# Regrouping the readers of the transposed input, the loads of the opening, and one step of the query rotation

## The chip, the cores and the metric

The kernel runs on one core of a Trainium2 chip. The metric is the device time of one execution in microseconds, the median over several runs. The engines are TensorE (PE; weight loads are listed as PEld), VectorE (DVE), ScalarE (ACT), GpSimd (POOL), and the queues that start transfers, above all SyncE's (SP).

## The reference, cut to what matters

A two-layer encoder over 512 tokens of width 1024. Layer 0 is a combined input projection that feeds two groups of attention heads, layer 1 a neighbourhood attention; each is followed by a squared-ReLU MLP. The change lies in layer 0, in its first part:

```python
hn = rmsnorm(h, norm_mix[layer])
z = h @ w_in                                # here h is hn
qa, ka, va, cq, ckv, kr = jnp.split(z, EVEN_SPLITS, axis=-1)
qa = axial_rope(rmsnorm(qa.reshape(b, s, A_HEADS, HEAD_DIM), a_q_norm), row, col)
ka = axial_rope(rmsnorm(ka.reshape(b, s, A_KV_HEADS, HEAD_DIM), a_k_norm), row, col)
oa = block_attention(qa, ka, va, HEAD_DIM ** -0.5)
```

`rmsnorm` divides by the root of the mean square over the row; the rotation `axial_rope` mixes pairs of channels with cosine and sine tables.

## The kernel before, in words

Activations are kept channel-major: eight "row tiles" `hT[:, k, :]` of 128 channels by 512 tokens. Each fp32 matrix product is made of three single-pass products (`mm3`, lines 509 to 511): both operands are split into a rounded high part and the low remainder, and high x high, high x low and low x high are added in one PSUM bank. Splitting a weight chunk takes an ACT copy for the high part (line 212; line 210 on DVE for the first chunk) and a DVE subtraction for the low part (line 202).

**The opening.** The input x comes token-major in four column blocks (`load_x`, line 119; block 0 in two halves), each holding two row tiles. The first 384 used columns of the input projection come in eight chunks of 128 rows (`load_w`, loads at line 190, a ring of four `raw` buffers). `make_x(k)` has TensorE transpose row tile k into a PSUM bank of tag `t`, of which there are two (line 548), and then reads this bank four times: ACT rounds it times the norm's gain into the high part of `X[k]` (553), DVE makes the low part (554), ACT makes the square for the norm's sum (556), and DVE copies the tile to `hT` (557). The square is added to `acc` (560), on POOL, for the last tile on DVE. `use_w(k, m)` runs the three matmuls of row tile k and column group m; there are three groups with a bank each. Rounds k = 0 to 5 of `opening` hold the nine matmuls of tile k, and the transposes of tile k+2 among them. Then tiles 6 and 7 follow group by group (`last_rows`), with the norm's sum between (`compact_r`, line 530: products of `acc` with a column of ones), a transpose of small gain vectors (1133), and then `others`, the product for three further tiles of 128 queries. Inside `opening` the order of PE, ACT, DVE and POOL is that of the program; the SP queue's order, and all engines' before the opening, come from a planner that works with estimated times. It also makes two engines that read one PSUM bank do so one after the other, in the program's order.

**The attention of the first group.** Eight heads in pairs, four units of 128 queries each, counted by `n` in `step`. In each unit TensorE makes the scores (1004), DVE and ACT the softmax (1008, 1010), TensorE transposes the result three units later (979), ACT and DVE split that (981, 982), and after each odd unit's transposes the product with the values follows one unit later (992). Between the units `fill` puts matmuls of other products. The rotation of the next pair of query tiles comes in two steps: `rope_q` at the pair's start (POOL and SP transfers), and `sum_q`, which adds the two halves (663), splits them (665, 666) and sends parts to their partitions (667 to 669, SP). `scales` makes the norms of queries of tiles 1 to 3 from sums gathered in a staging bank of tag `t` in units 0 to 2: an ACT copy (586), four transposes (589) and sixteen small DVE operations (592 to 596, 159 to 169, 688). The order in the attention is the planner's.

Of the kernel before, what the change touches and what calls it, by code (L numbers as in the profile page):

```python
# [19 lines left out]
KD = D // P  # L20
# [10 lines left out]
def f32(ap):  # L31
    return ap.bitcast(F32)
# [3 lines left out]
def encoder_kernel(ctx: ExitStack, tc: tile.TileContext, ins, out, dbg=None):  # L36
# [54 lines left out]
    def scratch(dt=F32):  # L91
        return scp.tile([P, 512], dt, tag="sc", name=nm("sc"))
# [24 lines left out]
    def load_x(q, z=None):  # L117
        a, m = (0, 256) if z is None else (128 * z, 128)
        SP.dma_start(xq[q].t.rearrange("p (j d) -> p j d", j=4)[:, :, a : a + m],
                     xv[:, :, 256 * q + a : 256 * q + a + m])  # L120
# [12 lines left out]
    def idle_work(n, b=None):  # L133
        b = b or ob()
        for _ in range(n):
            PE.matmul(b[:, 0:P], ones, ones, start=True, stop=True)
# [8 lines left out]
    def gmix(l, k):  # L145
        return gT[:, 8 * l + k : 8 * l + k + 1]
# [36 lines left out]
    def chunk(parts, nk, ncol, heads=None, eng=None, first=False):  # L183

        raw = wp.tile([P, 1024], F32, tag="raw", bufs=4, name=nm("raw"))
        r3 = raw[:, 0 : nk * ncol].rearrange("p (k n) -> p k n", k=nk)
        for lo, n, src in parts:
            dst = r3[:, :, lo : lo + n]
            if len(src.shape) == 3:
                SP.dma_start(dst, src)  # L190
            else:
                for k in range(nk):
                    SP.dma_start(dst[:, k].rearrange("p (z m) -> p z m", z=src.shape[2]), src[:, k])
        yield
        hi = wp.tile([P, 1024], F32R, tag="whi", name=nm("whi"))
        lo_ = wp.tile([P, 1024], F32R, tag="wlo", name=nm("wlo"))
        m = nk * ncol
        v = lambda t: t[:, 0:m].rearrange("p (k n) -> p k n", k=nk)
        lows = []

        def low(to, src, high):
            z = lambda: (eng or DVE).tensor_tensor(to, src, f32(high), op=ALU.subtract)  # L202
            if eng:
                z()
            else:
                lows.append(z)

        if heads is None:
            if first:
                DVE.tensor_copy(hi[:, 0:m], raw[:, 0:m])  # L210
            else:
                ACT.activation(hi[:, 0:m], raw[:, 0:m], AF.Copy)  # L212
            low(lo_[:, 0:m], raw[:, 0:m], hi[:, 0:m])
        else:

            na, nb = heads
            hn = ncol // (na + nb)
            r4 = r3.rearrange("p k (h e) -> p k h e", h=hn)
            for e0, n, o in ((0, na, 0), (na, nb, hn * na)):
                z = [v(t)[:, :, o : o + hn * n].rearrange("p k (h e) -> p k h e", h=hn) for t in (hi, lo_)]  # L220
                src = r4[:, :, :, e0 : e0 + n]
                ACT.activation(z[0], src, AF.Copy)
                low(z[1], src, z[0])
        yield v(hi), v(lo_), lows
# [319 lines left out]
    def make_x(k):  # L544
        b = stb()
        for j in range(4):
            o = 256 * j + P * (k % 2)
            PE.transpose(b[:, j * P : (j + 1) * P], xq[k // 2].t[:, o : o + P], ident)
        order = lambda z: z.rearrange("p (c r) -> p c r", r=ROWS)
        bt = b.rearrange("p (r c) -> p c r", r=ROWS)  # L550
        x3 = X[k].t.rearrange("p (a c r) -> p a c r", a=2, r=ROWS)
        g = gmix(0, k)
        ACT.activation(x3[:, 0], bt, AF.Copy, scale=g)
        DVE.scalar_tensor_tensor(x3[:, 1], bt, g, f32(x3[:, 0]), op0=ALU.mult, op1=ALU.subtract)  # L554
        sq = acc if k == 0 else scratch()
        ACT.activation(order(sq), bt, AF.Square)
        DVE.tensor_copy(order(hT[:, k, :]), bt)
        if k:

            (DVE if k == KD - 1 else POOL).tensor_tensor(acc, acc, sq, op=ALU.add)  # L560
# [121 lines left out]
    hold = {}  # L682
# [77 lines left out]

    def load_w(k):
        w = rows(w_in, k, 1)
        _, (hi, lo, lows) = chunk([(0, 256, w[:, :, 512:768]), (256, 128, w[:, :, 0:128])], 1, 384, first=k == 0)
        for z in lows:
            z()
        W[k] = hi, lo
# [5 lines left out]
    load_x(0, 0)  # L772
    load_w(0)
    load_x(0, 1)
    load_w(1)
    load_x(1)
    make_x(0)
    idle_work(4)
    make_x(1)
    load_w(2)  # L780
    load_x(2)

    kst = Slot()

# [246 lines left out]
    def heads_A():  # L1031
        for h in range(8):
            t, e, kv = h // 2, h % 2, h // 4
            if e == 0 and t < 3:
                rope_q(t + 1)
            q, k = QA[t].pair(), KA[kv].pair()

            def done(i, t=t, e=e):
                if e == 1 and t < 3 and i == 0:
                    sum_q(t + 1)  # L1040
                if i == 3 and e:
                    QA[t].free()
                    if t % 2:
                        KA[t // 2].free()

            yield dict(e=e, done=done, scale=lambda i, h=h: scA[h][:, i : i + 1],
                       passes=lambda i, q=q, k=k, e=e: [(q[:, e, i * P : (i + 1) * P], k[:, z, :]) for z in range(2)],
                       vlhs=lambda kt, kv=kv: VAv[:, kt, kv, :], after=VA.free if h == 7 else lambda: None)
# [35 lines left out]
    def step(h, i):  # L1084
        n = count[0]
        count[0] += 1
        if n < 3:

            if n == 0:
                hold["stq"] = stb()  # L1090
            stat(hold[f"sq{n + 1}"], n, 3, ind1(n + 1)[:, 2:8], hold["stq"], 6)
            if n == 2:
                scales(hold["stq"], 6, "rsQ", 2, 6)
        if n == 35:

            ok = [s_.pair() for s_ in O]
            assert len(ok) == 4
            fill.add(*out_proj(w_out, 0, ok, [0, 1, 2], "out"))
            projB(1, True)
            fill.add(*out_proj(w_out, 0, ok, [3, 4, 5], "out"))  # L1100
            fill.add(*out_proj(w_out, 0, ok, [6, 7], "out"))
        fill.run(1.5)
# [11 lines left out]
    def opening():  # L1114
        for k in range(6):
            use_w(k, 0)
            if k == 0:
                load_x(3)
            make_x(k + 2)
            use_w(k, 1)  # L1120
            use_w(k, 2)
            if k + 3 < KD:
                load_w(k + 3)
            if k == 2:
                SP.dma_start(rpA.t, ins["cst"][:, C_ROPE : C_ROPE + 2 * S])
            if k == 3:
                preload(1)
            if k == 4:
                preload(2)
        weights(0, 0)  # L1130
        SP.dma_start(rpB.t, ins["cst"][:, C_ROPE + 2 * S : C_ROPE + 4 * S])
        gp = stb()
        PE.transpose(gp[:, 0:31], gs.t[32:63, 0:P], ident[32:63, 32:63])
        DVE.tensor_copy(gT[:, 16:47], gp[:, 0:31])

        def last_rows(m):
            for k in (6, 7):
                use_w(k, m)

        last_rows(0)  # L1140
        sqk, low_k = squares(banks[0])
        kg, sh, krot = scratch(), scratch(), Slot(F32)
        ACT.activation(kg, banks[0], AF.Copy, scale=gT[:, 46:47])
        DVE.tensor_copy(r0, compact_r(acc))
        DVE.tensor_tensor(r0sq, r0, r0, op=ALU.mult)
        last_rows(2)
        ev_q(0, banks[2])
        low_k(DVE)
        hold["low"](DVE)
        last_rows(1)  # L1150
        q0 = first_q()
        next(q0)
        va = ev_va(banks[1])
        for n, _ in enumerate(others):
            if n == 0:
                next(va)
                DVE.stream_shuffle(sh, kg, sw16)
                DVE.tensor_tensor(kg, kg, cosA, op=ALU.mult)
                DVE.tensor_tensor(sh, sh, sinA, op=ALU.mult)
                DVE.tensor_tensor(krot.t[:, 0:S], kg, sh, op=ALU.add)  # L1160
            elif n == 2:
                st = stb()
                stat(sqk, 0, 2, ind1(1)[:, 0:4], st, 4)
            elif n == 3:
                stat(hold["sq0"], 1, 2, ind1(0)[:, 0:4], st, 4)
            elif n == 5:
                rs = scales(st, 4, "rsA", 0, 2)
                ka = keys(krot, rs[:, :, 2:4])
                next(ka)
            elif n == 7:  # L1170
                next(va)
            elif n == 13:
                next(ka)
                next(q0)
                next(ka)
            elif n == 14:
                next(va)
                next(q0)
        for _ in range(3):
            next(first_z)  # L1180
# [694 lines left out]
```

## Time and profile before

| | |
|---|---|
| median of 3 runs | 1180.86 us (1178.01 to 1181.37) |
| the profiled execution | 1179.42 us, span 1177.6 us |
| mean granted TensorE clock | 0.996 |
| PE busy | 1156.2 us, 98% of the span |
| DVE busy | 898.7 us, 76% |
| ACT busy | 646.7 us, 55% |
| POOL busy | 549.6 us, 47% |

Rows of the timeline give the start, the duration, the engine, the line, the operation with its output and inputs, and in brackets how long the engine stood idle before it and what ended that. Rows of waits give the total, the number and the longest. The granted clock is a share of full speed.

### The profile page before, as it was taken

How to read it: one execution, taken by the hardware profiler on the slowest of the kernel's cores; microseconds unless marked ns; L12 is line 12 of the kernel's file. 1: busy time of each engine (PE TensorE's matmuls, PEld its weight loads, DVE VectorE, ACT ScalarE, POOL GpSimd, SP SyncE). 2: the span in 40 equal slices, each digit the busy share in tenths (PEclk: the TensorE clock that was granted, in tenths of full speed). 3: DMA queues.
4: the chain of work that ended last, by engine and by line, in shares of the span. 5: the costliest groups of instructions: out<-in, count | busy, mean ns of one | idle time of the engine just before them, and what ended most of it. 6: DMA issues, size and time to landing. Idle time of an engine off the chain costs nothing. (4 is left out here: it accounts for less than half of the span.)

```text
span 1177.6 us, 20064 instructions
## 1 busy us (share of the span) xinstructions
PE 1156.2 (98%) x7212; PEld 1021.2 (87%) x7212; DVE 898.7 (76%) x1540; ACT 646.7 (55%) x1106; POOL 549.6 (47%) x684
## 2 busy tenths in 40 slices
PE   8999999999999999999999999999999999999997
PEld 6777788888898999989998998988889899998995
DVE  6878998878876587798884676667987678779775
ACT  4667676764444456743453555555553366663344
POOL 4257242315452878429802232221357558825920
PEclk9999999999999999999999999999999999999999
DMA  7323314222435623225226465433243223342322
GB/s 207 98 73 93 90 50 135 72 64 81 149 91 174 191 76 95 89 91 162 72 73 174 126 172 137 128 105 117 90 153 108 81 73 92 90 131 75 126 73 72
DMA packets 113476, 128.04 MB, mean 109 GB/s; under 512 B 9332, under 2 KB 92193, under 8 KB 113377
## 3 DMA queue, kind: packets, MB, share of 16 engines
q1 hardware_dynamic: 110320, 119.30, 34.0%
q0 software_dynamic: 2304, 6.31, 2.3%
q8 instruction: 57, 0.93, 0.3%
q10 hardware_dynamic: 752, 1.15, 0.3%
q14 instruction: 43, 0.34, 0.1%
HBM read 104.32 MB, written 6.29 MB: 94 GB/s over the span
## 5 line engine op out<-in xcount | busy, mean ns | idle before, releaser
L312 DVE TENSOR_TENSOR wlo<-a,whi 128x896 fp32r<-128x896 f32 x133 | 164.4, 1241 | 77.3 <-ACT whi L311 74.2
L311 ACT ACTIVATE whi<-a 128x896 fp32r<-128x896 f32 x133 | 125.7, 949 | 154.1 <-PE s L397 28.1
L509 PE MATMUL mm<-a,whi 128*128 128x512 f32 x473 | 192.1, 408 | 0.8 <-ACT a L840 0.5
L510 PE MATMUL mm<-a,whi 128*128 128x512 f32 x473 | 187.6, 397 | 0.5 <-DVE a L554 0.4
L511 PE MATMUL mm<-a,wlo 128*128 128x512 f32 x473 | 187.2, 397 | 0.0
L202 DVE TENSOR_TENSOR wlo<-raw,whi 128x1024 fp32r<-128x1024 f32 (+4 forms) x117 | 136.7, 1173 | 48.9 <-ACT whi L212 46.4
L305 POOL TENSOR_TENSOR a<-a 128x128 f32<-128x128 f32 x133 | 88.2, 663 | 137.9 <-DMA a<-in_ffn_w_up_dram 74.3
L212 ACT ACTIVATE whi<-raw 128x1024 fp32r<-128x1024 f32 (+3 forms) x120 | 113.1, 945 | 66.5 <-PE s L510 18.8
L306 POOL TENSOR_TENSOR a<-a 128x256 f32<-128x256 f32 x133 | 129.0, 970 | 10.4
L307 POOL TENSOR_TENSOR a<-a 128x128 f32<-128x128 f32 x133 | 116.0, 872 | 10.4
L398 PE MATMUL mm<-a,wlo 128*128 128x256 f32 x390 | 109.6, 281 | 1.3 <-DVE wlo L312 1.3
L396 PE MATMUL mm<-a,whi 128*128 128x256 f32 x390 | 109.5, 281 | 0.0
L397 PE MATMUL mm<-a,whi 128*128 128x256 f32 x390 | 109.1, 280 | 0.0
L509 PEld LDWEIGHTS mm<-a,whi 128*128 128x128 f32 x473 | 89.2, 189 | 20.9 <-issue 1.4
L511 PEld LDWEIGHTS mm<-a,wlo 128*128 128x128 f32 x473 | 89.1, 188 | 20.5
L510 PEld LDWEIGHTS mm<-a,whi 128*128 128x128 f32 x473 | 89.5, 189 | 18.4 <-DVE a L554 1.2
L1531 POOL TENSOR_SCALAR p<-p,ti 128x256 f32<-128x256 f32 x64 | 35.6, 567 | 105.2 <-DVE ti L1530 91.8
L1012 POOL TENSOR_SCALAR p<-p,ti 128x512 f32<-128x512 f32 x64 | 45.2, 708 | 83.7 <-DVE ti L1011 66.3
L396 PE MATMUL t<-a,whi 128*128 128x256 f32 x280 | 78.6, 281 | 0.0
L397 PE MATMUL t<-a,whi 128*128 128x256 f32 x280 | 78.3, 280 | 0.0
L398 PE MATMUL t<-a,wlo 128*128 128x256 f32 x280 | 78.3, 280 | 0.0
L398 PEld LDWEIGHTS mm<-a,wlo 128*128 128x128 f32 x390 | 73.4, 188 | 2.1 <-DVE wlo L312 2.1
(354 smaller groups left out, 3260.5 us busy)
## 6 DMA issues: line engine op xcount, KB each, us to landing
a<-in_ffn_w_up_dram SPq DMA_DIRECT2D x100, 256.0 KB
raw<-in_ffn_w_down_dram SPq DMA_DIRECT2D x42, 512.0 KB
a<-in_ffn_w_down_dram SPq DMA_DIRECT2D x33, 256.0 KB
raw<-in_od_w_qkv_dram SPq DMA_DIRECT2D x64, 128.0 KB
raw<-in_ffn_w_up_dram SPq DMA_DIRECT2D x12, 512.0 KB
a<-a SPq DMA_DIRECT2D x18, 256.0 KB
bias<-bx SPq DMA_DIRECT2D x16, 256.0 KB
raw<-in_od_w_qkv_dram SPq DMA_DIRECT2D x8, 512.0 KB
```

The source lines that it names most:

```text
L202: z = lambda: (eng or DVE).tensor_tensor(to, src, f32(high), op=ALU.subtract)
L212: ACT.activation(hi[:, 0:m], raw[:, 0:m], AF.Copy)
L306: POOL.tensor_tensor(r[:, 4:6], r[:, 2:3].to_broadcast([P, 2, P]), r[:, 0:7:6], op=ALU.add)
L307: POOL.tensor_tensor(r[:, 7], r[:, 3], r[:, 5], op=ALU.subtract)
L311: ACT.activation(hi[:, 0:896], raw[:, 128:1024], AF.Copy)
L312: DVE.tensor_tensor(lo[:, 0:896], raw[:, 128:1024], f32(hi[:, 0:896]), op=ALU.subtract)
L396: PE.matmul(o, wh, x[:, 0], start=kp == 0 and n in (0, 1, 3, 5), stop=False, skip_group_check=True)
L397: PE.matmul(o, wh, x[:, 1], start=False, stop=False, skip_group_check=True)
L398: PE.matmul(o, wl, x[:, 0], start=False, stop=kp == self.np - 1, skip_group_check=True)
L509: PE.matmul(o, wh, xh, start=first, stop=False)
L510: PE.matmul(o, wh, xl, start=False, stop=False)
L511: PE.matmul(o, wl, xh, start=False, stop=last)
```

## The change

- In `make_x`, for tiles 2 to 7, the square (ACT) stands right after the rounding (ACT), ahead of DVE's two reads. For tiles 0 and 1 the square comes last and reads the copy in `hT` instead of the bank.
- Loading a weight chunk and splitting it are separate steps. Chunks 0 to 3 and all x blocks are asked for before the first split, so that chunk 3 stands ahead of x block 3; in the opening chunk k+4 is asked for in round k, where it was k+3. The load of the rotary table (line 1125) comes after round 3's weight load, instead of after round 2's.
- In round 0 the transposes of tile 2 stand behind all nine matmuls, instead of behind the first three.
- `sum_q` comes at the second unit of the pair's second head, instead of the first.
- `scales` for the query tiles 1 to 3 comes at unit 3, instead of unit 2. The staging bank is taken as before.

```diff
@@ make_x
         g = gmix(0, k)
+        sq = acc if k == 0 else scratch()
         ACT.activation(x3[:, 0], bt, AF.Copy, scale=g)
+
+        if k > 1:
+            ACT.activation(order(sq), bt, AF.Square)
         DVE.scalar_tensor_tensor(x3[:, 1], bt, g, f32(x3[:, 0]), op0=ALU.mult, op1=ALU.subtract)
-        sq = acc if k == 0 else scratch()
-        ACT.activation(order(sq), bt, AF.Square)
         DVE.tensor_copy(order(hT[:, k, :]), bt)
+        if k < 2:
+            ACT.activation(sq, hT[:, k, :], AF.Square)
@@ load_w
-        _, (hi, lo, lows) = chunk([(0, 256, w[:, :, 512:768]), (256, 128, w[:, :, 0:128])], 1, 384, first=k == 0)
+        W[k] = chunk([(0, 256, w[:, :, 512:768]), (256, 128, w[:, :, 0:128])], 1, 384, first=k == 0)
+        next(W[k])
+
+    def split_w(k):
+        hi, lo, lows = next(W[k])
         for z in lows:
             z()
         W[k] = hi, lo
@@ before the opening
     load_x(0, 1)
-    load_w(1)
-    load_x(1)
+    for k in (1, 2, 3):
+        load_w(k)
+        load_x(k)
+    split_w(0)
     make_x(0)
     idle_work(4)
+    split_w(1)
     make_x(1)
-    load_w(2)
-    load_x(2)
+    split_w(2)
@@ heads_A, done
-                if e == 1 and t < 3 and i == 0:
+                if e == 1 and t < 3 and i == 1:
                     sum_q(t + 1)
@@ step
+        if n == 0:
+            hold["stq"] = stb()
         if n < 3:
-
-            if n == 0:
-                hold["stq"] = stb()
             stat(hold[f"sq{n + 1}"], n, 3, ind1(n + 1)[:, 2:8], hold["stq"], 6)
-            if n == 2:
-                scales(hold["stq"], 6, "rsQ", 2, 6)
+        if n == 3:
+            scales(hold["stq"], 6, "rsQ", 2, 6)
@@ opening
             use_w(k, 0)
-            if k == 0:
-                load_x(3)
-            make_x(k + 2)
+            if k:
+                make_x(k + 2)
             use_w(k, 1)
             use_w(k, 2)
+            if k == 0:
+                make_x(2)
+            if k + 4 < KD:
+                load_w(k + 4)
             if k + 3 < KD:
-                load_w(k + 3)
-            if k == 2:
+                split_w(k + 3)
+            if k == 3:
                 SP.dma_start(rpA.t, ins["cst"][:, C_ROPE : C_ROPE + 2 * S])
-            if k == 3:
                 preload(1)
```

## The prediction

> **What bounds the kernel now.** I read the page's engine shares first, then TensorE's own waits, then windows over the part that the change touches, then the timeline inside those windows.
>
> ```profile
> PE 1156.2 (98%) x7212; PEld 1021.2 (87%) x7212; DVE 898.7 (76%) x1540; ACT 646.7 (55%) x1106; POOL 549.6 (47%) x684
> PE o L992 <- DVE a L982: 2.1, 3, 1.7
> PE t L548 <- DVE hT L557: 1.8, 2, 1.4
> PE t L530 <- DVE acc L560: 1.4, 1, 1.4
> PE t L1133 <- issue: 1.1, 1, 1.1
> PE mm L510 <- DVE a L554: 0.4, 1, 0.4
> ```
>
> TensorE is busy 98% of the span, so only its idle time and its clock can be won, and no wait of its list is on a DMA: time won early should reach the end. Of its waits, lines 548, 530, 1133 and the one on 554 (510) lie in the opening, and 992 lies in the attention that follows. The opening by windows, cut at the start of each group of transposes (length, TensorE's busy time and instructions, its granted clock, DMA share, GB/s; the last two rows give the other engines too, before the clock):
>
> ```profile
> 7.23:9.86 2.63, 1.21 (x6) 1.00 0.96 314
> 9.86:12.45 2.59, 2.56 (x13) 1.00 1.10 355
> 12.45:14.98 2.53, 2.53 (x14) 1.00 1.03 321
> ...
> 17.52:20.52 3.00, 2.71 (x15) 1.00 0.48 117
> 20.52:23.69 3.17, 2.72 (x13) 1.00 0.71 216
> 23.69:26.77 3.08, 2.02 (x11) 1.00 0.48 133
> 26.77:30.59 3.82, 2.06 (x7) 1.00 0.54 157
> 30.59:35.88 5.29, 5.29 (x20) 0.68 0.26 76
> 36.00:60.00 24.00, 24.00 (x111) 18.61 (x110) 20.21 (x43) 14.67 (x27) 6.91 (x5) 1.00 0.35 97
> 60.00:145.00 85.00, 82.44 (x464) 65.29 (x462) 70.17 (x178) 59.05 (x125) 44.37 (x48) 1.00 0.32 84
> ```
>
> One round of the opening (nine matmuls and four transposes) takes 2.53 us where TensorE doesn't wait, and 3.00 to 3.17 later. The last window runs at a clock of 0.68. From 36 to 60 TensorE never idles; from 60 to 145 it idles 2.56 us. Why the later rounds take longer shows in one of them, row tile 5's on DVE, ACT and POOL:
>
> ```profile
> 20.33 1.19 DVE L202 TENSOR_TENSOR wlo<-raw,whi 128x384 fp32r<-128x384 f32 x1
> 21.45 0.74 DVE L554 SCALAR_TENSOR_TENSOR a<-t,gT,a 128x512 fp32r<-128x512 f32 x1
> 22.22 0.60 ACT L556 ACTIVATE sc<-t 128x512 f32<-128x512 f32 x1 [1.54 <-DVE a L554]
> 22.85 0.69 DVE L557 COPY hT<-t 128x512 f32<-128x512 f32 x1 [0.66 <-ACT sc L556]
> 22.96 1.27 POOL L560 TENSOR_TENSOR acc<-acc,sc 128x512 f32<-128x512 f32 x1 [1.85 <-ACT sc L556]
> 23.46 1.19 DVE L202 TENSOR_TENSOR wlo<-raw,whi 128x384 fp32r<-128x384 f32 x1
> 23.69 0.63 PE L548 MATMUL t<-cst,a 128*128 128x128 f32 x4 [0.45 <-DVE hT L557]
> ```
>
> The bank is read by ACT (rounding, 553), DVE (554), ACT (square, 556), DVE (copy, 557), in that order. The square needs nothing that 554 makes and still waits for it: readers of one bank on two engines go one after the other. So DVE stands still for the square, 0.66 us, in the middle of its own chain: 20.33 to 23.46 is 3.13 us, the round's length. There are two banks, so tile k+2's transposes wait for tile k's copy. Beyond that the POOL addition (1.27) covers DVE's weight split 202, which then takes 1.19 where it takes 0.56 alone:
>
> ```profile
> 7.86 0.56 DVE L202 TENSOR_TENSOR wlo<-raw,whi 128x384 fp32r<-128x384 f32 x1
> 9.89 0.63 PE L548 MATMUL t<-cst,a 128*128 128x128 f32 x4 [1.39 <-DVE hT L557]
> 14.04 0.53 ACT L212 ACTIVATE whi<-raw 128x384 fp32r<-128x384 f32 x1 [1.05 <-DMA raw<-in_ev_w_in_dram]
> 15.66 0.39 PE L510 MATMUL mm<-a,whi 128*128 128x512 f32 x1
> 15.89 0.39 PE L511 MATMUL mm<-a,wlo 128*128 128x512 f32 x1
> 20.00 0.68 ACT L553 ACTIVATE a<-t,gT 128x512 fp32r<-128x512 f32 x1
> 29.76 0.68 DVE L560 TENSOR_TENSOR acc<-acc,sc 128x512 f32<-128x512 f32 x1
> 33.01 0.63 PE L510 MATMUL mm<-a,whi 128*128 128x512 f32 x1
> 33.44 0.63 PE L511 MATMUL mm<-a,wlo 128*128 128x512 f32 x1
> 35.91 1.31 POOL L644 TENSOR_TENSOR sc<-a,a 128x512 f32<-128x512 f32 x1 [8.55 <-ACT a L631]
> ```
>
> Matmuls start 0.23 us apart (15.66, 15.89), and 0.43 apart in the slow stretch (33.01, 33.44).
>
> **The change, part by part.**
>
> *Tile 2's transposes behind six more matmuls.* In round 0 they stand ahead of products 1 and 2 and wait 1.39 us for tile 0's copy, which was behind its square. Now all nine matmuls come first (6 x 0.23 = 1.40 us fill the gap), and the copy precedes the square, which reads SBUF. The transposes then could start at 9.65; their x data was there at 9.86 at the latest, perhaps not sooner, so the gain is 1.2 to 1.4; I take 1.2.
>
> *The new order of readers.* ACT rounds and squares, then DVE subtracts and copies: one hand-over instead of three. DVE's round is 0.56 + 0.74 + 0.69 = 1.99 us, since the POOL addition now starts when the square ends and lies beside 554 and 557, not beside 202. ACT's round is 0.53 + 0.68 + 0.60 = 1.8. Both are under TensorE's 2.53, so rounds run at 2.53: the windows 17.52, 20.52 and 23.69 give back 0.47 + 0.64. No row shows 554 beside a busy POOL; were it and the copy stretched by all that 202 loses (0.63), DVE's round is 2.62 and five rounds lose 0.4. The other bound is none; 557 at 22.85 stays at 0.69 beside POOL, so I take none. The price: tile k's low part comes 0.6 us later after its high part. Its reader stands 1.5 rounds off, which covers it, except in the tail (below).
>
> *Loads.* The queue takes w3 ahead of x3, and each later w one round sooner; the four raw buffers allow that as soon as the split of w(k) is done. In the row at 14.04 ACT waited 1.05 us for w3 behind x3's 512 KB; at 321 to 355 GB/s that is 1.5 us, so w3 lands near 12.5, and x3, late by w3's 192 KB (0.6 us), is wanted only by round 4. ACT's queue holds tile 3's rounding behind w3's split: with w3 at 12.5, X3 is complete at 15.0 and wanted at 15.5. If w3 came no sooner, TensorE would wait about 1.0 there. I take 0.1. The rotary table's 512 KB and the two preloads move behind w7; the table's first reader, 644, starts at 35.91 and waited for ACT, not for a DMA. Hidden.
>
> *Tail.* Tile 7's transposes come at 9.85 + 1.15 + 4 x 2.53 = 21.1 instead of 23.69. Behind them: rounding 0.68, square 0.60, 554 0.74, copy 0.69, acc 0.68 and hand-overs, so acc is ready at about 25.0. TensorE has 23.0 + 0.14 (line 1133, which no longer waits 1.06, its bank being free) + 6 x 0.23 = 24.55, and no longer waits 0.4 for 554. It stalls some 0.55 for acc and starts line 530 at 25.1, against 30.59: 5.5 us won.
>
> *Clock.* After 29.2 TensorE had no wide matmul until 31.48, and then ran eight at 0.43: 8 x 0.2 = 1.6 us lost, 0.1 of it in the turn, say 1.5. The thin stretch is now 24.55 to 26.0, 1.45 us; the quiet 1.39 us before 9.89 took no clock (1.00 in both windows beside it). So I take the 1.5 as won. [...]
>
> Opening: 5.5 + 1.5 = 7.0 us, seen as the first matmul after the opening starting at 28.9 instead of 35.88. What follows (the rsqrt chain, key and query splits) hangs on 530 and on TensorE, with DVE busy 20.21 of 24 us: it loses 1.5 us of its lead, and TensorE's list shows no wait there, so I cost it at nothing.
>
> *Attention.* Two steps move one unit later: the query scales (one ACT copy, four transposes, sixteen small DVE operations), and a pair's sum (two DVE, one ACT, three SP transfers).
>
> ```profile
> 68.61 1.12 DVE L663 TENSOR_TENSOR sc<-sc,sc 128x512 f32<-128x512 f32 x1 [0.21 <-issue]
> 69.66 1.27 DVE L167 TENSOR_TENSOR ti<-ti,ti 128x24 f32<-128x24 f32 x1
> 71.62 0.68 DVE L666 TENSOR_TENSOR sc<-sc,a 128x512 fp32r<-128x512 f32 x1
> 72.31 0.68 DVE L982 TENSOR_TENSOR a<-t,a 128x512 fp32r<-128x512 f32 x1
> 73.04 1.09 PE L992 MATMUL o<-a,a 128*128 128x256 f32 x7 [1.72 <-DVE a L982]
> SPq L894 <- DVE ti L169: 12.3, 1, 12.3
> ```
>
> The transposes made in unit 4 are those of unit 1, an odd one, and the values product in unit 5 wants them. Their low part 982 ran at 72.31, behind 663 (1.12), a step of the scales (1.27) and 666 (0.68), and TensorE stood 1.72. With the sum in unit 5 it collides with an even unit's transposes, wanted two units later. The scales then crowd units 3 to 6 as before, one later, and their staging bank is held one unit longer, so unit 4's transposes wait for unit 3's 982: at worst 0.7, that instruction's time, is lost. At best the 2.1 of TensorE's list is won. I take 1.3, nearer to the upper end, because 663 and 666 alone (1.80) are longer than the 1.72 that TensorE stood. The transfers of the sum land one unit later, under a lead of three units. SP order: they pass a unit's weight loads, which wait for buffers anyway.
>
> Sum: 7.0 + 1.3 = 8.3. The profiled execution took 1179.42 (span 1177.6 and 1.8 around it), giving 1171.1; it stands 1.4 below the median of the three, from which the sum gives 1172.6. I say 1172.
>
> **Rivals.**
> 1. *A part stays.* The clock halves again after the thin stretch (1.5 lost), or w3 lands no sooner (1.0), or nothing comes in attention (1.3); two of these give 1174 to 1177. For it: acc is still the last gate. Against: its stall is a third of the old one.
> 2. *DVE stays the bound* through POOL, 2.62 a round, and the rsqrt and key steps behind it turn the lost lead into waits: of 7.0 some 3 stay, 1177.5 to 1180. Against: 557 unstretched at 22.85. [...] No run yet shows 554 beside POOL.
> 3. *The attention's order.* It is laid out by a planner, not by hand, and shifted inputs re-lay it. If it puts a matmul ahead of a transfer whose queue stands still (the row of line 894: 12.3 us), the gain is gone: 1179.4 - 7.0 + 12.3 = 1184.7. It decides from 10 us of new waits on. Against: now 2.56 us idle in 85.
> 4. *No effect*: readers were not the gate, the x loads were: then rounds stay at 3.1 and TensorE still waits, about 1179. Against: DMA share falls to 0.48 in the slow rounds.
>
> **How the numbers follow.** Forecast (1168.5 to 1174) 0.60; rival 1 0.20; rivals 2 and 4 0.13, a fifth of it still faster by over 0.3%; rival 3 0.07. A change under 0.3% (3.5 us) can't be told from none here. Faster 0.82, same 0.12, slower 0.06. The range 1168 to 1177.5 takes in the forecast and rival 1.
>
> **What would show it.** Squares of line 556 without waits on 554; rounds at 2.53 to the last; 202 at 0.56 throughout; line 530 near 25 us, its wait under 0.6; clock 1.00 from 25 to 30; the 992 wait of 1.7 gone. Wrong: first matmul of the next product later than 31; or TensorE idle over 3 us between 50 and 140.

## The result, and the profile after

The changed kernel takes 1171.82 us (median of 6 runs, 1171.13 to 1172.23) against 1179.43 for the kernel before on the same chip (1177.3 to 1181.37): a ratio of 0.9936, with a 95% interval of 0.9921 to 0.9951. The forecast was 1172.0, in a range of 1168 to 1177.5. The profiled execution took 1172.23 us; its span is 7.2 us shorter than before's.

The engines' busy time on the page of the changed kernel (us, share of the span, instructions):

```profile
PE 1154.3 (99%) x7212; PEld 1021.0 (87%) x7212; DVE 898.3 (77%) x1540; ACT 647.2 (55%) x1106; POOL 547.8 (47%) x684
```

TensorE is still the bound, as before. Line numbers below 550 are unchanged, later ones have moved: in `make_x` the rounding 553 is now 554, DVE's low part 554 is 558, the copy 557 is 559, the square 556 is 557 (from the bank) or 561 (from `hT`), and the addition 560 is 564; 992 is now 1003, 982 is 993, 1008 is 1019, 1133 is 1146, 663 and 666 are 667 and 670. Of TensorE's own waits (us in all, how many, the longest) these are the counterpart of the prediction's list:

```profile
PE o L1003 <- ACT a L992: 0.5, 1, 0.5
PE t L548 <- DMA a<-in_x_dram: 0.4, 1, 0.4
PE s L1015 <- DMA a<-sc: 0.3, 1, 0.3
PE mm L510 <- DMA raw<-in_ev_w_in_dram: 0.2, 1, 0.2
PE o L1003 <- DVE a L993: 0.2, 1, 0.2
PE t L530 <- DVE acc L564: 0.2, 1, 0.2
```

Nothing above 0.5 us is left of the waits that the change was about. In their place stand small ones on DMA. The opening of the changed kernel in windows (length, TensorE's busy time and instructions, clock, DMA share, GB/s), cut at the transposes of tiles 2, 4, 5, 6 and 7, at the small transpose, at line 530 and at the first matmul of the next product:

```profile
8.05:10.24 2.19, 2.19 (x13) 1.00 1.09 344
10.24:14.48 4.24, 4.01 (x21) 1.00 0.87 267
14.48:17.07 2.59, 2.59 (x15) 1.00 0.12 26
17.07:19.64 2.57, 2.57 (x15) 1.00 0.88 229
19.64:22.17 2.53, 2.53 (x14) 1.00 1.09 384
22.17:24.10 1.93, 1.93 (x11) 1.00 0.94 353
24.10:26.11 2.01, 1.84 (x8) 1.00 0.81 220
26.11:29.87 3.76, 3.76 (x20) 1.00 0.43 133
```

And the attention's stretch of the same kernel, with all engines:

```profile
54.00:139.00 85.00, 83.82 (x472) 66.78 (x471) 71.06 (x181) 60.57 (x128) 44.69 (x49) 1.00 0.33 85
```

The rounds of 3.00 and 3.17 us are gone; the last window, 5.29 us at a clock of 0.68 before, is 3.76 at 1.00. The next product starts at 29.87 instead of 35.88, which is 6.0 us of the 7.2. In the attention's stretch TensorE idles 1.18 of 85 us instead of 2.56.

A ledger of the rest comes from the first DVE operation of each attention unit's softmax (1008, now 1019): its start in the changed kernel minus its start before.

| at unit | 0 | 4 | 8 | 23 | 24 | 28 | 40 | 63 | end of the span |
|---|---|---|---|---|---|---|---|---|---|
| changed kernel minus before, us | -6.0 | -8.6 | -8.3 | -8.7 | -5.5 | -7.1 | -7.4 | -7.3 | -7.2 |

So the opening brings 6.0, units 3 to 8 bring 2.2 more, and around unit 24 some 0.9 is lost again.

### The profile page after: what moved, and what is told of

It is laid out like the page before. It is cut to its first block, busy times and chain, and to the rows that moved or that the text cites. A ratio compares the mean times of both kernels' runs of the same rounds, so it can differ in the third digit from the quotient of the medians.

```text
span 1170.4 us, 20069 instructions
## 1 busy us (share of the span) xinstructions
PE 1154.3 (99%) x7212; PEld 1021.0 (87%) x7212; DVE 898.3 (77%) x1540; ACT 647.2 (55%) x1106; POOL 547.8 (47%) x684
## 5 line engine op out<-in xcount | busy, mean ns | idle before, releaser
L305 POOL TENSOR_TENSOR a<-a 128x128 f32<-128x128 f32 x133 | 90.2, 678 | 140.1 <-DMA a<-in_ffn_w_up_dram 95.1
L306 POOL TENSOR_TENSOR a<-a 128x256 f32<-128x256 f32 x133 | 123.4, 928 | 10.4
L307 POOL TENSOR_TENSOR a<-a 128x128 f32<-128x128 f32 x133 | 116.7, 878 | 10.4
```

The source lines that it names most:

```text
L306: POOL.tensor_tensor(r[:, 4:6], r[:, 2:3].to_broadcast([P, 2, P]), r[:, 0:7:6], op=ALU.add)
L307: POOL.tensor_tensor(r[:, 7], r[:, 3], r[:, 5], op=ALU.subtract)
```

## The experiments

Twelve runs, each timed against the kernel before on its own chip; medians of before lie between 1179.1 and 1181.3 there. "Opening" below is the stretch from the transposes of tile 1 to the first matmul of the next product: 29.0 us before (6.87 to 35.88) and 22.2 in the changed kernel (7.67 to 29.87).

**The new order of readers alone, and its undoing.** `make_x` of the changed kernel in the kernel before; and the old `make_x` in the changed kernel (the diff is cut to the reads):

```diff
         ACT.activation(x3[:, 0], bt, AF.Copy, scale=g)
+        if k > 1:
+            ACT.activation(order(sq), bt, AF.Square)
         DVE.scalar_tensor_tensor(x3[:, 1], bt, g, f32(x3[:, 0]), op0=ALU.mult, op1=ALU.subtract)
-        ACT.activation(order(sq), bt, AF.Square)
         DVE.tensor_copy(order(hT[:, k, :]), bt)
+        if k < 2:
+            ACT.activation(sq, hT[:, k, :], AF.Square)
```

> The kernel before with the new order of the bank's four readers alone (old loads, old place of tile 2's transposes, old attention). Theory A, the hand-overs between ACT and DVE were the gate of the opening: rounds 4 and 5 fall from 3.0 and 3.2 to 2.6 us or less, the wait for acc falls under 0.7 us, the clock no longer halves, and the first matmul after the opening comes at 31 us or sooner instead of 35.88; the run is 4 to 6 us faster. Rival B, the loads were the gate: rounds stay near 3.1 us and the run gains under 1.5 us.

> The changed kernel with the old order of readers put back (new loads, new places, new attention). Theory A: rounds 4 and 5 are at 3.1 us again, acc is late by over 1 us, the clock halves again, and the first matmul after the opening comes at 33.5 us or later instead of 29.87; 4 us or more slower than the changed kernel. Rival B: it comes by 31 us and the run loses under 1.5 us.

The order alone: 1175.45 us, ratio 0.9962 (0.9948 to 0.9976); its median is 3.8 us below that of before, a little less than the 4 to 6 expected. Undone in the changed kernel: 1177.41, ratio 0.9982 (0.9971 to 0.9994). First the windows of the order alone (tile 2's round, rounds 4 and 5 with the tail, and from line 530 on), then those of the changed kernel with the old order:

```profile
9.29:11.85 2.56, 2.56 (x13) 1.00 1.08 355
19.45:21.98 2.53, 2.53 (x14) 1.00 0.94 334
21.98:25.92 3.94, 3.77 (x18) 1.00 0.64 195
25.92:29.69 3.77, 3.77 (x20) 1.00 0.34 106
```

```profile
17.34:20.42 3.08, 2.73 (x13) 1.00 0.70 205
20.42:23.59 3.17, 2.73 (x13) 1.00 0.87 291
23.59:30.49 6.90, 4.09 (x17) 0.89 0.51 152
30.49:36.72 6.23, 6.23 (x20) 0.57 0.22 64
```

Theory A holds on both sides: with the new readers the rounds are at 2.53 and the clock at 1.00 whatever the loads are; with the old ones they are at 3.08 and 3.17 again and the clock is down. The opening takes 22.8 us (6.87 to 29.69) and 29.6 us (7.13 to 36.72). The four readers' order is the opening's whole gain, and the rival of the loads is out. The two parts of that edit, the square ahead of DVE's reads for tiles 2 to 7 and the square from `hT` for tiles 0 and 1, were not run apart.

**Tile 2's transposes and the loads.** Two more undoings in the changed kernel:

```diff
@@ tile 2's transposes in their old place
-            if k:
-                make_x(k + 2)
+            make_x(k + 2)
...
-            if k == 0:
-                make_x(2)
@@ the old loads
-    for k in (1, 2, 3):
-        load_w(k)
-        load_x(k)
+    load_w(1)
+    load_x(1)
...
+            if k == 0:
+                load_x(3)
...
-            if k + 4 < KD:
-                load_w(k + 4)
             if k + 3 < KD:
+                load_w(k + 3)
                 split_w(k + 3)
```

> The changed kernel with tile 2's transposes back between the first three and the other six matmuls of round 0. If the place matters as the prediction has it: a wait of 0.6 to 1.4 us stands before those transposes, and the first matmul after the opening comes that much later than 29.87. Rival: the wait is only moved, since the later rounds wait for loads or for the readers instead; the opening ends within 0.3 us of the changed kernel's.

> The changed kernel with the old order of loads (chunk 3 behind x block 3, one round less ahead, rotary table after round 2's load). The prediction's step: chunk 3 lands 1.5 us later and TensorE waits about 1 us in round 3. Rival, the loads of the new order only crowd the first ones: the first matmul of the opening comes at 7.3 us as before the change instead of 8.05, and the opening ends 0 to 0.8 us sooner than the changed kernel's.

Both are no effect: 1172.32 us with a ratio of 0.9936 (0.9919 to 0.9954), and 1172.26 with 0.9936 (0.9920 to 0.9952). The openings take 21.95 us (7.90 to 29.85) and 22.07 (7.84 to 29.91). The transposes of tile 2, in the old place, in the timeline of the kernel with the order alone (start, duration, and in brackets the idle time ahead):

```profile
9.29 0.63 PE L548 MATMUL t<-cst,a 128*128 128x128 f32 x4 [0.79 <-DMA a<-in_x_dram]
```

There they waited for x itself, since that execution had its tile 1 early (6.87). In two other profiles with the old place and the new readers they start at 9.36, after a wait of 0.38 for the copy, and at 9.45, only 0.3 behind the matmul ahead of them (9.15). Over all profiles tile 1's transposes start anywhere from 6.54 to 7.92 us, with old loads (6.87, 7.34, 7.84, 7.92) as with new ones (6.54, 7.13, 7.73, 7.90), while with the new readers the opening ends at 29.35 to 29.91 us in every one. The early starts were spent on waiting. The rival's 0.8 us for crowded loads was this spread, and is out too. The load of chunk 3 was waited for by ACT in the kernel with the old loads (13.77, its timeline below), and TensorE did not feel it:

```profile
13.77 0.53 ACT L212 ACTIVATE whi<-raw 128x384 fp32r<-128x384 f32 x1 [0.73 <-DMA raw<-in_ev_w_in_dram]
```

**The clock.** Six products of ones in the kernel before, where TensorE stood idle ahead of line 530:

```diff
         last_rows(0)
+        idle_work(6)
         sqk, low_k = squares(banks[0])
```

> The kernel before with six products of ones (128 columns each, about 1.5 us of TensorE work that nothing uses) put behind the matmuls of tiles 6 and 7 of the first group, where TensorE stood before line 530; nothing else is changed and the wait for acc stays. Theory A, the quiet stretch halves the clock: it stays at 1.00 from 30 to 36 us, the ten matmuls behind run at 0.23 instead of 0.43 us, and the run is 1.2 to 1.8 us faster than before. Rival, the clock falls for another reason (the one-column products themselves, or the time): the clock is halved again and the run is within 0.5 us of before.

1178.36 us, ratio 0.9986 (0.9975 to 0.9997). The windows (all engines; the clock is the third number from the right):

```profile
29.00:32.00 3.00, 2.96 (x23) 2.71 (x24) 2.26 (x4) 2.32 (x5) 0.00 (x0) 1.00 0.50 131
32.00:35.50 3.50, 3.50 (x16) 2.82 (x17) 3.07 (x17) 2.48 (x5) 0.18 (x1) 1.00 0.42 115
```

The clock stays at 1.00, and from line 530 to the next product it takes 3.77 us (30.95 to 34.72) instead of 5.29: 1.52 won with useless work in a gap that stays as long. The gap is filled in one profile; in two that have it open, before and the old order in the changed kernel, the windows from line 530 on show 0.68 and 0.57. So of the opening's gain 1.5 is clock and the rest the waits themselves. The median moved by less than that (0.8 us); the interval holds both.

**The attention's two steps, alone and undone.** Both in the kernel before, and both undone in the changed one:

```diff
-                if e == 1 and t < 3 and i == 0:
+                if e == 1 and t < 3 and i == 1:
                     sum_q(t + 1)
...
-            if n == 2:
-                scales(hold["stq"], 6, "rsQ", 2, 6)
+        if n == 3:
+            scales(hold["stq"], 6, "rsQ", 2, 6)
```

> The kernel before with the two steps of the attention moved one unit later, the opening as before. Theory A: units 0 to 8 take 22.3 us instead of 24.5, as in the changed kernel, 0.9 us is given back where the third pair's scores begin (unit 24), and the run is 1.3 us faster, give or take 0.7. Rival C, the wait of 1.7 us was lost through the changed opening and not through the moved steps: it stays, and the run is within 0.5 us of before.

> The changed kernel with both steps of the attention in their old places. Theory A: the 1.7 us wait of the values product is back, unit 24 loses nothing, the run is 1.3 us slower than the changed kernel, give or take 0.7. Rival C: the wait does not return, the run is within 0.5 us.

Alone they give 1177.95 us, ratio 0.9980 (0.9969 to 0.9991); in the ledger 2.2 us from unit 0 to unit 8, and 1.8 by unit 63. Undone, 1176.22, ratio 0.9962 (0.9947 to 0.9977): by the medians 4.4 us above the changed kernel (3.1 by the two ratios), far over the 1.3 expected. The 1.7 us wait is back, and behind it this stands (timeline of TensorE, then windows of the same execution, then those of the kernel before at the same wait):

```profile
66.96 1.10 PE L1003 MATMUL o<-a,a 128*128 128x256 f32 x7 [1.71 <-DVE a L993]
68.26 0.63 PE L510 MATMUL mm<-a,whi 128*128 128x512 f32 x1
```

```profile
66.00:68.00 2.00, 1.04 (x8) 1.04 (x9) 2.00 (x9) 1.02 (x4) 0.70 (x1) 0.99 0.83 264
68.00:70.00 2.00, 2.00 (x7) 1.52 (x6) 0.82 (x4) 0.63 (x2) 0.69 (x1) 0.50 0.18 54
70.00:72.00 2.00, 2.00 (x7) 1.54 (x6) 0.00 (x0) 0.00 (x0) 0.00 (x0) 0.66 0.32 74
```

```profile
72.00:74.00 2.00, 0.96 (x8) 0.96 (x9) 2.00 (x9) 1.02 (x4) 0.70 (x1) 1.00 0.84 263
74.00:76.00 2.00, 2.00 (x11) 1.64 (x10) 0.91 (x4) 0.72 (x2) 0.70 (x1) 1.00 0.18 60
```

Behind the same wait, 1.71 and 1.72 us, the clock was 0.50 in one execution and 1.00 in the other (and the order alone, with the attention as before, is 6.2 us ahead of before at unit 63, as at the opening's end): between units 5 and 6 the kernel with the steps undone loses 1.6 us against before, with no idle time to show for it. That explains 1.6 of the 3.1 us that were not expected. The other 1.5 appears after the attention and is not explained. One of this kernel's eight runs took 1172.53, the seven others 1176.03 to 1176.67, so part of the loss comes and goes.

**Which of the two steps, and what unit 24 waited for.** In the changed kernel: the third pair's sum back in the old place; the scales back; all three sums back.

```diff
@@ third pair's sum back
+                if e == 1 and t < 3 and i == (t < 2):
@@ scales back
+            if n == 2:
+                scales(hold["stq"], 6, "rsQ", 2, 6)
@@ all sums back
+                if e == 1 and t < 3 and i == 0:
```

> The changed kernel with the third pair's sum at the old place (first unit of the pair's second head), the first two pairs' sums one unit later. Theory A, the later sum of the third pair is what unit 24 waited for: the lead over before does not fall from 8.7 to 5.5 us between units 23 and 24, 0.6 to 1.0 us less is given back by unit 36, and the run is 0.6 to 1.0 us faster than the changed kernel. Rival: the planner re-lays out the stretch anyway and the lead falls as before; within 0.3 us.

> The changed kernel with the query scales back in unit 2; the pairs' sums stay one unit later. Theory A, the sum's three operations in front of the values product's input are the 1.7 us wait: units 3 to 8 gain the 2.2 us over before as in the changed kernel, within 0.5 us of it. Rival, the sixteen small operations are what fills DVE there: a wait of 1 us or more stands in unit 5 or before, and units 3 to 8 gain under 1.2 us.

> The changed kernel with all three sums back in the first unit, the query scales still one unit later. Theory A: a wait of 1 us or more stands before the values product of unit 5, units 3 to 8 gain under 1.2 us over before, unit 24 loses nothing. Rival: no wait over 0.6 us, units 3 to 8 gain over 1.7 us. If TensorE stands over 1.4 us, the clock may halve behind it, which costs 1.5 us more.

| kernel | won, units 0 to 8 | won, units 0 to 63 | us | ratio |
|---|---|---|---|---|
| changed kernel | 2.2 | 1.3 | 1171.82 | 0.9936 |
| third pair's sum back | 2.2 | 2.2 | 1171.77 | 0.9934 (0.9918 to 0.9950) |
| scales back | 0.9 | 0.3 | 1173.80 | 0.9940 (0.9922 to 0.9959) |
| all sums back | 2.2 | 2.2 | 1171.44 | 0.9921 (0.9901 to 0.9941) |

Here theory A fell: with the sums moved and the scales not, a wait of 1.1 us stays; with the scales moved and the sums not, it is gone. DVE's timeline in the first of these (in this and the next fences rows between are left out):

```profile
62.96 1.24 DVE L166 TENSOR_TENSOR ti<-ti 128x24 f32<-128x24 f32 x1
64.12 0.74 DVE L1019 CUSTOM_DVE_ANT_0 p<-s,zeros,scA 128x512 f32<-128x512 f32 x1
65.09 0.68 DVE L993 TENSOR_TENSOR a<-t,a 128x512 fp32r<-128x512 f32 x1
```

TensorE's wait for that split in the list of waits of the same kernel:

```profile
PE o L1003 <- DVE a L993: 1.1, 1, 1.1
```

And DVE's timeline in the second, with the sums back:

```profile
63.17 0.68 DVE L993 TENSOR_TENSOR a<-t,a 128x512 fp32r<-128x512 f32 x1
66.66 0.69 DVE L667 TENSOR_TENSOR sc<-sc,sc 128x512 f32<-128x512 f32 x1
```

With the scales in unit 2 the small operations, one of them at 1.24 where most take 0.17 or 0.18, stand ahead of the split 993 that the values product wants. With the scales in unit 3 the split comes first, and the planner puts even an early sum 667 behind it by itself. The third pair's low half (666, now 670) shows what the later sum costs: in the changed kernel, then with that sum back:

```profile
124.11 0.83 DVE L670 TENSOR_TENSOR sc<-sc,a 128x512 fp32r<-128x512 f32 x1
131.97 0.75 DVE L1019 CUSTOM_DVE_ANT_0 p<-s,zeros,scA 128x512 f32<-128x512 f32 x1
```

```profile
121.02 0.69 DVE L670 TENSOR_TENSOR sc<-sc,a 128x512 fp32r<-128x512 f32 x1
128.82 0.73 DVE L1019 CUSTOM_DVE_ANT_0 p<-s,zeros,scA 128x512 f32<-128x512 f32 x1
```

The split comes 3.1 us later, and unit 24 starts 3.15 us later; most of that is filled with other matmuls meanwhile, and 0.9 is lost. The 0.9 is back by unit 63 with the third sum back, but the 0.6 to 1.0 us expected of the whole run did not come: 1171.77 against 1171.82.

**Two edits alone.** The kernel before with the order of readers and the scales in unit 3, beside the changed kernel again:

> The kernel before with two of the edits alone: the new order of readers and the query scales in unit 3. If these two make the whole gain: counted from the first tile 1 transposes, the opening ends within 0.8 us of the changed kernel's 22.2 us, units 3 to 8 gain 2.2 us over before, unit 24 loses nothing, and the run is as fast as the changed kernel or up to 1 us faster. If the places and the loads carry a part: the opening is over 1 us longer and the run slower by as much.

> The changed kernel itself, on the same chip as the run with two edits alone, for their comparison: 1171.8 us, give or take 0.7.

1173.05 us, ratio 0.9942 (0.9926 to 0.9957), and 1172.34, ratio 0.9937 (0.9922 to 0.9952). The opening ends at 29.77 us in both; the attention wins 1.85 us by unit 63 with two edits and 1.3 with all. The two edits are the gain, as far as the runs can tell: the medians differ by 0.7 us and the intervals overlap. No version was shown to beat the changed kernel: the one with all sums back has the lowest ratio, but 0.9921 and 0.9936 lie inside each other's intervals.

## Why the prediction was right, and where not

*The order of readers, right in mechanism and size.* No square of line 557 (the bank's square) waits for DVE's 558, rounds run at 2.53 to 2.59. Forecast from tile 1's transposes to the next product: 6.87 to 28.9, 22.0 us; measured 22.2, and 22.06 to 22.08 in the five other profiles that have the new readers and tile 2's new place and start at 7.28 or later. The 6.0 in place of 7.0 is the execution's start, 0.8 later at 7.67, which the profiles show to vary by 1.4 us on its own. That an earlier start would have won the rest is not shown: the changed kernel again started at 6.54, tile 2's transposes stood until 10.21, long after the copy that their bank needed (done at 7.98), and the next product came at 29.77. The earliest in ten profiles with the new readers is 29.35, so 28.9 was never reached. A further 0.4 went in round 2, as the changed kernel's timeline shows:

```profile
10.89 0.52 ACT L212 ACTIVATE whi<-raw 128x384 fp32r<-128x384 f32 x1 [1.04 <-DMA raw<-in_ev_w_in_dram]
11.89 0.62 ACT L561 ACTIVATE sc<-hT 128x512 f32<-128x512 f32 x1
12.41 0.59 ACT L557 ACTIVATE sc<-t 128x512 f32<-128x512 f32 x1
13.04 0.75 DVE L558 SCALAR_TENSOR_TENSOR a<-t,gT,a 128x512 fp32r<-128x512 f32 x1 [1.03 <-ACT sc L557]
13.84 0.50 PE L510 MATMUL mm<-a,whi 128*128 128x512 f32 x1 [0.23 <-DMA raw<-in_ev_w_in_dram]
```

ACT waited 1.04 us for weight chunk 2, and tile 2's rounding stands behind that split; tile 1's square (561) then stands ahead of tile 2's square. So tile 2's low part was ready at 13.8, and TensorE's second matmul of round 2 stood until 13.84 for it (put down to a DMA, but the chunk's split had been done at 12.0). Tile 4's transposes come 3.10 us behind tile 3's here and 3.01 in the changed kernel again, where ACT waited 1.54 for the chunk; in the five profiles just named, with the same order on ACT and the chunk there sooner, they come 2.68 behind. So the late chunk cost the 0.4; what the place of tile 1's square costs, at most the 0.15 from 2.53 to 2.68, was not tried. The tail was better than forecast: line 530 waited 0.17, not 0.55.

*POOL beside DVE's bank reads.* Taken as no cost, and so it is: tile 4's are the pair at 17.31, with POOL busy until 18.54, and of DVE's operations here only one split 202 is stretched, to 1.36 where the other seven take 0.54 to 0.56 (DVE's timeline of the changed kernel):

```profile
14.30 1.36 DVE L202 TENSOR_TENSOR wlo<-raw,whi 128x384 fp32r<-128x384 f32 x1
16.84 0.54 DVE L202 TENSOR_TENSOR wlo<-raw,whi 128x384 fp32r<-128x384 f32 x1
17.31 0.74 DVE L558 SCALAR_TENSOR_TENSOR a<-t,gT,a 128x512 fp32r<-128x512 f32 x1
17.97 0.68 DVE L559 COPY hT<-t 128x512 f32<-128x512 f32 x1
```

POOL's timeline over the same time, the four additions together and then the second and the fourth alone:

```profile
12.60 5.94 POOL L564 TENSOR_TENSOR acc<-acc,sc 128x512 f32<-128x512 f32 x4 [7.13 <-ACT sc L561]
13.96 1.29 POOL L564 TENSOR_TENSOR acc<-acc,sc 128x512 f32<-128x512 f32 x1
16.91 1.63 POOL L564 TENSOR_TENSOR acc<-acc,sc 128x512 f32<-128x512 f32 x1
```

In two pairs one of the two was held up: the split that began beside a running addition (14.30) ended at 15.66, 0.41 behind the addition's end at 15.25, as in the kernel before (21.52 behind 21.12); the split that began first (16.84) kept its 0.54, and the addition that began beside it at 16.91 took 1.63 instead of 1.29. 558 and 559, which read the bank, took 0.74 and 0.68 beside POOL (17.31, 17.97), and 0.75 and 0.68 at 9.37 and 10.04, where POOL stood idle until 12.60. What sets the split apart from them was not tried. "202 at 0.56 throughout" was wrong for one of the eight.

*The clock, right*: 1.5 us, shown by the filled gap. Behind the attention's wait of 1.7 us it was 0.50 in the kernel with the two steps undone and 1.00 in the kernel before; what decides between the two is not shown.

*Tile 2's transposes, mis-sized*: 1.2 us forecast, 0 measured. The wait that the sum took from the old trace was the copy behind the square, and the readers' order had already removed most of it; what was left there was x's arrival or 0.38 of the copy. So the 1.2 was credited to the wrong edit: without it the forecast had 5.8 for the opening, and the order alone, which starts at 6.87 like before, comes to the next product 6.2 sooner (29.69).

*The loads, mis-sized in their bounds*: 0.1 taken and up to 1.0 allowed, for chunk 3; 0 measured. The chunk that did cost something, 0.4 in both profiles of the changed kernel, was chunk 2, which the sum does not have.

*Attention, the right sum by the wrong step*: 1.3 forecast, 1.3 measured by unit 63. The step that failed is "663 and 666 alone (1.80) are longer than the 1.72 that TensorE stood": the scales' move alone brought the 2.2 us by unit 8, the sums' move alone 0.9, and both together no more than the scales' alone; what stood ahead of the split were the scales' small operations. And "The transfers of the sum land one unit later, under a lead of three units" failed for the third pair, which lost 0.9. The two errors cancelled, which is luck.

*The number*: the forecast took 8.3 us off; the span fell by 7.2 and the median by 7.6. That 1172 came within 0.2 us is in part luck, since it started from a median of three, 1180.86, and a profile 1.4 below it, while the median of six is 1179.43.

*A sum of the rivals is off*: two of rival 1's three parts (1.5, 1.0, 1.3) add to 2.3 to 2.8 us, which gives 1174.3 to 1174.8 from the 1172.0 forecast, not 1174 to 1177. The range's upper end was wider than its parts.

*Afterwards* the lead is not simply kept. Two kernels that were 8.7 us ahead at unit 63 (third sum back, all sums back) end 7.6 and 8.2 ahead, one that was 6.2 ahead (the order alone) ends 4.6 ahead. The MLP's waits for the low part of its weights (line 398, weight loads and matmuls counted together, for the split of line 312) differ from profile to profile there, 4.8 us in all in one and 7.8 in the order alone, 6.4 before; what sets them was not tried, and about 1 us of the attention's differences disappears in it.

## What to carry to other kernels

When two engines read one bank, count the hand-overs, not the reads: put each engine's reads together, and let a read that can take a copy in SBUF leave the bank. A wait in a trace belongs to the program that it was seen in; before counting two edits' gains together, ask whether the first removes the second's wait. Where an instruction queues behind several others, undo the moves one at a time before naming the one that mattered.

## What the runs showed of the hardware

Behind a TensorE wait of 1.71 us the granted clock was 0.50 from 68 to 70 us and 0.66 from 70 to 72 in one profile (both steps undone), and behind the same wait of 1.72 it stayed at 1.00 in the kernel before; so here such a wait cost either itself or itself and 1.6 us more. That the idle time is the cause was tried, by filling it, for the opening's gap alone. The changed kernel, whose profile shows neither the wait nor a halving (1.00 in its windows above), spreads little (1171.13 to 1172.23), and the kernel before, which has this wait and the opening's of 1.4, widely (1177.66 to 1184.05 in one set of 27 runs). The mean granted clock of each of these runs goes with its time: the eight runs at 0.995 or less took 1179.50 to 1184.05, the fourteen at 0.997 or more 1177.66 to 1180.96. So the clock goes with most of this spread; which wait it fell behind in which run is not on record.
